# Six raw weight buffers in place of four, four tiles fewer in the common pool, and one addition of a join moved up

## The chip, the cores and the metric

The kernel runs on one core of one Trainium2 chip. The metric is device time in microseconds (us) of one execution, as the median of several runs. TensorE multiplies matrices, VectorE (DVE in the rows) and ScalarE (ACT) work elementwise, GpSimd (POOL) does little here, and SyncE (SP) issues nearly all transfers from the chip's memory.

## The reference

One decoder layer on 256 tokens of width 2048, in float32. Two feed-forward layers of inner width 5632 stand around a mixer (sparse attention and a recurrent branch); this is the part that the change is about:

```python
def swiglu(h, w_in, w_out):
    a, b = jnp.split(h @ w_in, 2, axis=-1)
    return (jax.nn.silu(a) * b) @ w_out

h = layer_norm(DN_ALPHA * h + 0.5 * swiglu(h, ffn1_w_in[l], ffn1_w_out[l]), ln1_g[l], ln1_b[l])
# ... the mixer: q, k, v, indexer, gates, recurrence, three output products ...
h = layer_norm(DN_ALPHA * h + 0.5 * swiglu(h, ffn2_w_in[l], ffn2_w_out[l]), ln3_g[l], ln3_b[l])
```

## The kernel before

**Weights.** Every weight comes in pieces of 128 x 1024 float32 (512 KB). The class `Weights` handles a piece in three steps. `load_to` has SP issue the transfer into a tile named `raw` (`RAW_BUFS` = 4 of them, lines 192 and 206) or, for certain quarters of the feed-forward weights, into tiles named `k` (tags `k0` and `k1`, 4 and 3 of them, line 192). `split_to` turns the piece into a high part `wh` on ACT (line 300) and a low part `wl` = piece minus `wh` on DVE (line 301); there are five tiles of each (`HL_BUFS`). TensorE then takes three products for each operand: `wh` times high, `wl` times high, `wh` times low (lines 734, 735 and 736). A `raw` tile is free for the next transfer when the `wl` of its piece, or the last addition that reads it, has ended.

**Sums of quarters.** For three quarters of a feed-forward block's depth the kernel multiplies by sums of weight quarters instead of the plain quarters. These sums are made in place in the `k` tiles by DVE, `k += k` or `k += raw` (`add`, line 222), and are then split like any other piece. In the rows, `k<-k,raw` is such an addition.

**A feed-forward layer.** `blocksW` runs over 11 blocks of the inner width, in an order written out in `PLAN`: the products of forms P1, P2, Q3 to Q5, P6 and P7 (two groups of three matmuls to a piece), the plain pieces (`c`, twelve matmuls), and fills (`o`, twelve matmuls, line names `ob<-wh,gh`), which multiply the block before by the output weights. At the end of a block, `plain` joins it: two Silu on ACT, two additions `u` and `d` of a product sum in PSUM, two multiplications by the Silu (all lines 819). Just after it the next block's P1 sum is copied, negated, into a new PSUM tile by ACT (`mm<-bp`, line 819), and the form P6 adds to that tile (`mm<-wh,sh`).

**What sets the order.** TensorE, SP and GpSimd run in the order of the code. On DVE and ACT a scheduler sets the order at build time by priority and by its own estimate of when operands are ready; at run time each engine goes through its list in that order and waits where it must. SP too stands still at the first transfer whose tile isn't free, and all that are behind it wait with it.

**The common pool.** Tiles of 128 x 512 float32 that live for a while (activations, `sh`/`sl`, `zs`, `xg`, `vw`, `yr` and others) share one pool of `U_BUFS` = 53.

Of the kernel before, what the change touches and what calls it, by code (L numbers as in the profile page):

```python
# [12 lines left out]
OP = mybir.AluOpType  # L13
# [37 lines left out]

LAG = 2

U_BUFS = 53
T_BUFS = 8
RAW_BUFS = 4
K0_BUFS = 4
K1_BUFS = 3
HL_BUFS = 5
# [85 lines left out]
class Weights:  # L145
# [33 lines left out]
    def load_to(self, i):  # L179
        nc = self.nc  # L180
        while self.loaded <= min(i, len(self.pieces) - 1):
            ap, form = self.pieces[self.loaded]
            k = self.key(self.loaded)
            if isinstance(form, tuple):
                if form[0] in QUARTERS:
# [4 lines left out]
                    else:  # L190
                        t = self.pool.tile([P, PIECE], F32, name=f"raw{self.loaded}", tag="raw", bufs=RAW_BUFS)
                    nc.sync.dma_start(t, ap)
                    self.quarter[form[1], j] = t
            elif k not in self.raw:
# [5 lines left out]
                else:  # L200
                    t = self.pool.tile([P, PIECE], F32, name=f"raw{self.loaded}", tag="raw", bufs=RAW_BUFS)
                if form in QUADS.values():
# [52 lines left out]
    def small(self, name):  # L255
        return self.pool.tile([P, 512], F32, name=name, tag="u", bufs=U_BUFS)

# [119 lines left out]
def tile_layer(ctx, tc, x_fm, x_tm, pos, f1a, f1o, wA, wki, wB, wG, lru, lru_x, wab, wrb, wo, f2a, f2o,  # L377
# [5 lines left out]
    V, A, T, G = nc.vector, nc.scalar, nc.tensor, nc.gpsimd  # L383
    count = [0]

    def name(s):
        count[0] += 1
        return f"{s}{count[0]}"

    def U(s="u", dt=F32):  # L390
        return pool.tile([P, 512], dt, name=name(s), tag="u", bufs=U_BUFS)

# [12 lines left out]
    def CB():  # L405
        return psum.tile([P, 512], F32, name=name("mm"), tag="mm", bufs=2)
# [14 lines left out]
    def BP():  # L421
        return psum.tile([P, 512], F32, name=name("bp"), tag="bp", bufs=4)
# [303 lines left out]
    def blockB(x):  # L726
        ps = MM()
        for k in range(len(x)):
            mmB(ps, x[k], W.unit(P), k == 0, k == len(x) - 1)
        return ps  # L730

    def three(ps, xh, xl, w, start, stop, seeded=False):
        h, l = (v.rearrange("p (a h c) -> p a c h", h=2, c=P) for v in w)
        T.matmul(ps, xh, h, start=start, stop=False, skip_group_check=seeded)  # L734
        T.matmul(ps, xh, l, start=False, stop=False, skip_group_check=seeded)  # L735
        T.matmul(ps, xl, h, start=False, stop=stop, skip_group_check=seeded)  # L736

    def tokens(ps, x, t, w, start, stop, seeded=False):
        h, l = x(t) if callable(x) else (x[:, i, t * P:(t + 1) * P] for i in range(2))
        three(ps, h, l, w, start, stop, seeded)  # L740

    def eager(x, ps):

        ln, x.halves = x.halves, None
        W.step = 512
        base = W.cur + 1
        W.limit = base + AHEAD
        ws = []  # L750
        n = len(ps(0))
        for i in range(8):
            if i == 6:
                ln.half(1)
            ws.append(W.unit(512))
            tokens(ps(0)[i % n], ln.first[i // n], 0, ws[i], i < n, False)
        W.step = PIECE
        for i in range(8):
            tokens(ps(1)[i % n], x[i // n], 1, ws[i], i < n, False)
            if i % 2:  # L760
                W.split_to(base + AHEAD + 1 + i // 2)
        W.limit = None
# [45 lines left out]
    def xop(x, q, i, t):  # L808
        def op(r):
            v = x[4 * q + 2 * r + i]  # L810
            return v[:, 0, t * P:(t + 1) * P], v[:, 1, t * P:(t + 1) * P]
        return op

    def sop(forms, q, i):
        return lambda r: tuple(v[:, i * P:(i + 1) * P] for v in forms[2 * q + r])

    def urgent(f, *args, **kw):
        with tc.high_priority():
            f(*args, **kw)  # L819

    def blocksW(x, forms, fill, done):

        last = {(n, f): i for i, (n, f, k) in enumerate(PLAN)}
        bank = {n: {} for n in range(NBK)}
        z = {n: {} for n in range(NBK)}  # L830
        c = [None, None]

        def banks(t):
            if not c[t]:
                c[t] = [(CB, OB)[t]() for _ in range(2)]
            return c[t]

        def first(k, end):
            ws = [W.unit(512) for _ in range(2)]
            for t in range(2):  # L840
                for j in range(2):
                    tokens(banks(t)[j], x[k], t, ws[j], k == 0, k == NK - 1)
            for t in range(2 if end else 0):
                s = U("z")
                urgent(A.activation, s, c[t][0], AF.Silu)
                urgent(V.tensor_tensor, s, s, c[t][1], op=OP.mult)
                done(0, t, s)

        def plain(n, k, end):
            ws = [W.unit(512) for _ in range(2)]  # L850
            for t, j, b in ((0, 0, "B"), (0, 1, "D"), (1, 1, "A"), (1, 0, "E")):
                tokens(bank[n][b], x[k], t, ws[j], False, end, True)
            if end:
                v, ps = z[n], bank[n]
                s = [U("zs"), U("zs")]
                urgent(A.activation, s[0], ps["B"], AF.Silu)
                urgent(A.activation, s[1], ps["E"], AF.Silu)
                urgent(V.tensor_tensor, v["u"], ps["D"], v["u"], op=OP.add)
                urgent(V.tensor_tensor, v["u"], v["u"], s[0], op=OP.mult)
                done(n, 0, v["u"])  # L860
                urgent(V.tensor_tensor, v["d"], ps["A"], v["d"], op=OP.add)
                urgent(V.tensor_tensor, v["d"], v["d"], s[1], op=OP.mult)
                done(n, 1, v["d"])
                del bank[n], z[n]

        def product(n, form, k, end):
            b, op = {"P1": ("B", xop(x, k, 0, 0)), "P2": ("B", xop(x, k, 1, 0)), "Q3": ("D", sop(forms, k, 3)),
                     "Q4": ("E", xop(x, k, 1, 1)), "Q5": ("D", sop(forms, k, 0)), "P6": ("A", sop(forms, k, 1)),
                     "P7": ("A", sop(forms, k, 2))}[form]
            ps = bank[n]  # L870
            new = b not in ps
            if new:
                ps[b] = BP()
            for r in range(2):
                three(ps[b], *op(r), W.unit(512), new and r == 0, end and r == 1, form not in ("P1", "Q5"))
            if not end:
                return
            if form == "P1":
                ps["A"] = CB()
                urgent(A.activation, ps["A"], ps["B"], AF.Copy, scale=-1.0)  # L880
            elif form == "Q5":
                z[n]["d"] = U("zd")
                urgent(A.activation, z[n]["d"], ps["D"], AF.Copy)
            elif form == "P6":
                z[n]["u"] = U("zu")
                urgent(A.activation, z[n]["u"], ps["A"], AF.Copy)
            elif form == "P7":
                ps["E"] = CB()
                urgent(A.activation, ps["E"], ps["A"], AF.Copy, scale=-1.0)

        skip = 0
        if getattr(x, "halves", None):
            eager(x, banks)
            skip = 4
        for i, (n, form, k) in enumerate(PLAN):
            end = i == last[n, form]
            if i < skip:
                continue
            if form == "o":
                fill()  # L900
            elif n == 0:
                first(k, end)
            elif form == "c":
                plain(n, k, end)
            else:
                product(n, form, k, end)
# [18 lines left out]
    def column_block(x, forms, plan):  # L925


        if plan:
            return blockM(x, forms, plan)
        return [[p] for p in blockA(x)]  # L930
# [360 lines left out]
    qT, kT, v, qiT = [None] * 8, [None] * 2, [None] * 2, [None] * 4  # L1291
# [182 lines left out]
    for b in a_order:  # L1474
# [9 lines left out]
        ps = blockA(hs)  # L1484
# [16 lines left out]
    for nb in range(4):  # L1501
        if WGA and nb == WGA[0]:
            forms = make_forms(hs, QG)
        ps = column_block(hs, forms, MIXED["wG"].get(nb))
# [6 lines left out]
    for nb in range(4):  # L1511
        ps = column_block(ya, forms, MIXED["wab"].get(nb))
# [91 lines left out]
    for j in range(NR + LAG):  # L1604
# [5 lines left out]
        if j < NR:  # L1610
            ps = blockB(hs)
# [15 lines left out]
            ps = blockB(hs)  # L1627
# [3 lines left out]
        if j >= LAG:  # L1631
# [7 lines left out]
            if c == TPG - 1:  # L1639
                ps = BP()  # L1640
# [31 lines left out]
    for nb in range(4):  # L1672
        if WO and nb == 3:
            mforms = make_forms(mg, U)
        ps = column_block(yr, forms, MIXED["wrb"].get(nb))
        for t in range(2):
            d = gr[nb][t]
# [115 lines left out]
```

## Time and profile before

| | |
|---|---|
| runs | 2251.0, 2253.88, 2257.98 us (median 2253.88) |
| the profiled execution | 2250.04 us, of which its span is 2248.2 us |
| TensorE busy | 2219.8 us (99%) |
| DVE, ACT busy | 1958.7 us (87%), 1559.6 us (69%) |
| DMA | 459.33 MB, mean 204 GB/s |
| feed-forward layers | about 0 to 680 us and 1570 to 2240 us of the span |

A timeline row reads: start and duration in us, engine, line, operation, output <- inputs, shapes, count; in brackets the idle time of the engine just before it and what ended that. A row of waits reads: who waited, at which line, for whom: us in total, times, longest. Matmuls overlap: each lasts 0.38 us in the rows, but in an undisturbed stretch they start 0.216 us apart (0.21 and 0.22 in the rows), so TensorE's pace is read from the starts.

### The profile page before, as it was taken

What the parts mean: (1) busy time and instruction counts of PE and PEld (TensorE: products, weight loads), DVE (VectorE), ACT (ScalarE), POOL (GpSimd) and SP (SyncE); (2) the same over time, 40 slices, a digit from 0 to 9 for tenths busy, and PEclk for the clock granted to TensorE, in tenths of its full rate; (3) what the DMA queues carried; (4) which work ended last, traced back from release to release, by engine and by line L of the source; (5) the groups of instructions that cost most, each with busy time, mean ns of one, the idle gap of its engine ahead of it and who ended that gap; (6) DMA issues with size and microseconds to landing.
All of it is one profiled execution on the core that took longest, in us unless ns stands there. A gap on an engine that the chain in (4) does not pass through costs nothing.

```text
span 2248.2 us, 30930 instructions
## 1 busy us (share of the span) xinstructions
PE 2219.8 (99%) x11164; PEld 1939.3 (86%) x11164; DVE 1958.7 (87%) x2617; ACT 1559.6 (69%) x2222; POOL 22.4 (1%) x58
## 2 busy tenths in 40 slices
PE   9999999999999999999999999999999999999999
PEld 8888888888888888889999888898888888888887
DVE  7899999999988887678788886898999999999997
ACT  6777777777766556555688885555777777777774
POOL 0000000000001000000000000000000000000000
PEclk9999999999999999999999999999999999999999
DMA  8666655566666555566655566556666656665664
GB/s 302 215 225 218 205 192 203 197 204 215 211 206 219 175 182 164 161 214 199 209 177 188 184 203 235 194 194 195 215 220 210 219 199 223 220 209 193 206 213 157
DMA packets 133498, 459.33 MB, mean 204 GB/s; under 512 B 15040, under 2 KB 17856, under 8 KB 133344
## 3 DMA queue, kind: packets, MB, share of 16 engines
q1 hardware_dynamic: 130608, 449.37, 59.9%
q0 software_dynamic: 2160, 6.94, 1.0%
q8 instruction: 87, 1.43, 0.3%
q10 hardware_dynamic: 576, 1.05, 0.1%
q14 instruction: 67, 0.55, 0.1%
HBM read 455.20 MB, written 2.10 MB: 203 GB/s over the span
## 4 chain that ended last, share of the span: by engine, by line
PE 62%; DVE 17%; DMA 8%; issue 7%; ACT 5%; POOL 0%; ACTq 0%; SPq 0%; DVEq 0%; POOLq 0%
DVE wl L301 11%; PE ob L735 8%; PE ob L736 7%; PE ob L734 7%; PE mm L734 7%; PE mm L735 7%; PE mm L736 7%; DVE k L222 4%; DMA raw<-f2a 4%; DMA raw<-f1a 4%; PE bp L736 3%; PE bp L734 3%; PE bp L735 3%; ACT wh L300 3%; PE ob L723 2%
## 5 line engine op out<-in xcount | busy, mean ns | idle before, releaser
L301 DVE TENSOR_TENSOR wl<-raw,wh 128x1024 fp32r<-128x1024 f32 (+2 forms) x734 | 858.2, 1184 | 137.6 <-ACT wh L300 132.6
L300 ACT ACTIVATE wh<-raw 128x1024 fp32r<-128x1024 f32 (+2 forms) x734 | 741.4, 1025 | 320.0 <-PE mm L736 127.1
L301 DVE TENSOR_TENSOR wl<-k,wh 128x1024 fp32r<-128x1024 f32 x290 | 349.3, 1220 | 37.3 <-ACT wh L300 35.3
L300 ACT ACTIVATE wh<-k 128x1024 fp32r<-128x1024 f32 x290 | 302.7, 1056 | 112.4 <-DVE k L222 55.0
L735 PE MATMUL ob<-wl,gh 128*128 128x512 f32 x640 | 244.4, 382 | 9.8 <-DVE wl L301 9.8
L734 PE MATMUL ob<-wh,gh 128*128 128x512 f32 x640 | 244.6, 382 | 1.4 <-ACT ob L1226 1.4
L736 PE MATMUL ob<-wh,gl 128*128 128x512 f32 x640 | 242.7, 379 | 0.0
L222 DVE TENSOR_TENSOR k<-k,raw 128x1024 f32<-128x1024 f32 x174 | 211.6, 1219 | 32.0 <-DMA raw<-f1a 16.5
L734 PE MATMUL mm<-wh,hs 128*128 128x512 f32 x418 | 161.6, 387 | 0.0
L736 PE MATMUL mm<-wh,hs 128*128 128x512 f32 x418 | 158.5, 379 | 0.4 <-DVE hs L1054 0.4
L735 PE MATMUL mm<-wl,hs 128*128 128x512 f32 x418 | 158.5, 379 | 0.2 <-DVE wl L301 0.2
L735 PEld LDWEIGHTS ob<-wl,gh 128*128 128x128 f32 x640 | 121.0, 189 | 33.0 <-DVE wl L301 17.0
L734 PEld LDWEIGHTS ob<-wh,gh 128*128 128x128 f32 x640 | 121.0, 189 | 19.2 <-ACT ob L1226 2.8
L736 PEld LDWEIGHTS ob<-wh,gl 128*128 128x128 f32 x640 | 121.0, 189 | 17.1 <-DVE gl L819 0.5
L1238 ACT ACTIVATE y<-ob 128x512 f32<-128x512 f32 x152 | 89.5, 590 | 65.8 <-PE ob L736 65.7
L734 PE MATMUL ob<-wh,hs 128*128 128x512 f32 x304 | 118.4, 390 | 1.0 <-ACT hs L1053 1.0
L736 PE MATMUL ob<-wh,hs 128*128 128x512 f32 x304 | 115.5, 380 | 0.6 <-DVE hs L1054 0.6
L735 PE MATMUL ob<-wl,hs 128*128 128x512 f32 x304 | 115.2, 379 | 0.0
L723 PE MATMUL ob<-hs,wh 128*128 128x512 f32 x336 | 111.2, 382 | 0.0
L734 PE MATMUL bp<-wh,sh 128*128 128x512 f32 (+1 forms) x298 | 107.8, 362 | 1.3 <-ACT zd L819 1.3
L723 PE MATMUL mm<-hs,wh 128*128 128x512 f32 x320 | 106.7, 384 | 0.0
L735 PE MATMUL bp<-wl,sh 128*128 128x512 f32 (+1 forms) x298 | 106.1, 356 | 0.0
(404 smaller groups left out, 4828.2 us busy)
## 6 DMA issues: line engine op xcount, KB each, us to landing
raw<-f2a SPq DMA_DIRECT2D x118, 512.0 KB, 4.3
raw<-f1a SPq DMA_DIRECT2D x116, 512.0 KB, 4.5
raw<-f1o SPq DMA_DIRECT2D x88, 512.0 KB, 4.2
raw<-f2o SPq DMA_DIRECT2D x88, 512.0 KB, 3.7
raw<-wB SPq DMA_DIRECT2D x80, 512.0 KB, 4.5
raw<-wA SPq DMA_DIRECT2D x64, 512.0 KB, 3.5
raw<-wG SPq DMA_DIRECT2D x64, 512.0 KB, 3.6
k<-f1a SPq DMA_DIRECT2D x58, 512.0 KB, 6.9
```

Of the source, the lines that this page charges most:

```text
L222: self.nc.vector.tensor_tensor(v, v, self.quarter[q, j], op=OP.add)
L300: nc.scalar.activation(hp, src, AF.Copy)
L301: self.last = nc.vector.tensor_tensor(lp, src, hp, op=OP.subtract)
L723: T.matmul(ps, w[0], turns(x.rearrange("p a t -> p (a t)")), start=first, stop=False)
L734: T.matmul(ps, xh, h, start=start, stop=False, skip_group_check=seeded)
L735: T.matmul(ps, xh, l, start=False, stop=False, skip_group_check=seeded)
L736: T.matmul(ps, xl, h, start=False, stop=stop, skip_group_check=seeded)
L1238: A.activation(Y[t][nb], open_ps[t], AF.Copy, scale=0.5)
```

## The change

`RAW_BUFS` goes from 4 to 6, `U_BUFS` from 53 to 49 (a `raw` tile is twice as large as one of the pool, so the memory stays the same), and in the join the addition of `d` is written ahead of the addition of `u`.

```diff
-U_BUFS = 53
+U_BUFS = 49
 T_BUFS = 8
-RAW_BUFS = 4
+RAW_BUFS = 6
...
                 urgent(A.activation, s[1], ps["E"], AF.Silu)
+                urgent(V.tensor_tensor, v["d"], ps["A"], v["d"], op=OP.add)
                 urgent(V.tensor_tensor, v["u"], ps["D"], v["u"], op=OP.add)
                 urgent(V.tensor_tensor, v["u"], v["u"], s[0], op=OP.mult)
                 done(n, 0, v["u"])
-                urgent(V.tensor_tensor, v["d"], ps["A"], v["d"], op=OP.add)
                 urgent(V.tensor_tensor, v["d"], v["d"], s[1], op=OP.mult)
```

The order of TensorE, SP and GpSimd stays row for row. That of DVE and ACT is set by the scheduler. Three places of one block of the first feed-forward layer stand here (in the other blocks it is the same pattern); the numbers in the names tell tiles apart.

DVE, some pieces ahead of a join (`k_110`, `k_112`, `k_113` hold quarters, `raw_2120` is the quarter that two of them take up):

```order
 L301 TENSOR_TENSOR wl_2057<-k_110_1966,wh_2056 128x1024
 L301 TENSOR_TENSOR wl_2069<-k_113_2010,wh_2068 128x1024
+L222 TENSOR_TENSOR k_110_1966<-k_110_1966,raw_2120 128x1024
+L222 TENSOR_TENSOR k_113_2010<-k_113_2010,k_114_2022 128x1024
 L222 TENSOR_TENSOR k_108_1935<-k_108_1935,raw_2066 128x1024
-L222 TENSOR_TENSOR k_113_2010<-k_113_2010,k_114_2022 128x1024
+L222 TENSOR_TENSOR k_112_1997<-k_112_1997,raw_2120 128x1024
 L301 TENSOR_TENSOR wl_2094<-k_113_2010,wh_2093 128x1024
 L301 TENSOR_TENSOR wl_2104<-raw_2041,wh_2103 128x1024
```

Two additions more now stand ahead of `wl_2094`: four in a row in place of two.

DVE at the join itself, a few rows on:

```order
 L301 TENSOR_TENSOR wl_2133<-k_105_1898,wh_2132 128x1024
 L301 TENSOR_TENSOR wl_2147<-raw_2091,wh_2146 128x1024
-L222 TENSOR_TENSOR k_110_1966<-k_110_1966,raw_2120 128x1024
 L819 TENSOR_TENSOR zu_1797<-bp_1531,zu_1797 128x512
 L819 TENSOR_TENSOR zd_1635<-mm_1620,zd_1635 128x512
```

The addition of `raw_2120` is gone from ahead of the join. The join's additions stand as before, `u` first: the scheduler keeps that order in all 20 joins, so the line that the diff moves moves no instruction.

ACT at the same place, with what each row waits for (this order is the same before and after):

```order
L819 ACTIVATE zs_2179<-mm_1923 128x512 [waits PE_49]
L300 ACTIVATE wh_2188<-k_110_1966 128x1024 [waits DVE_49,Activation_49]
L819 ACTIVATE mm_2142<-bp_2009 128x512 [waits Activation_49]
L300 ACTIVATE wh_2204<-raw_2120 128x1024 [waits DMAHW2_49,PE_49]
L300 ACTIVATE wh_2218<-raw_2144 128x1024 [waits DMAHW3_49,PE_49]
```

Nothing moved here. The copy `mm_2142<-bp_2009` waits for ACT's own earlier rows alone, the last of which is the split of `k_110`, and that one waits for DVE's addition.

DVE ahead of the piece of a fill, some 20 us after the join:

```order
 L301 TENSOR_TENSOR wl_2310<-raw_2249,wh_2309 128x1024
-L222 TENSOR_TENSOR k_105_1898<-k_105_1898,raw_2216 128x1024
+L222 TENSOR_TENSOR k_110_1966<-k_110_1966,raw_2321 128x1024
 L301 TENSOR_TENSOR wl_2324<-k_108_1935,wh_2323 128x1024
-L222 TENSOR_TENSOR k_110_1966<-k_110_1966,raw_2321 128x1024
 L222 TENSOR_TENSOR k_113_2010<-k_113_2010,raw_2345 128x1024
 L301 TENSOR_TENSOR wl_2348<-raw_2280,wh_2347 128x1024
```

One addition has gone from here to an earlier row; the addition of `raw_2345` still stands right ahead of the fill's `wl_2348`.

## The prediction

> **What bounds the kernel now.** I read the busy times first, then who waited for whom on TensorE, then the timelines of DVE, ACT and SP around those waits, and last the DMA rates.
>
> ```profile
> PE 2219.8 (99%) x11164; PEld 1939.3 (86%) x11164; DVE 1958.7 (87%) x2617; ACT 1559.6 (69%) x2222; POOL 22.4 (1%) x58
> PE ob L735 <- DVE wl L301: 9.8, 16, 1.1
> PE mm L734 <- ACT mm L819: 5.5, 9, 1.2
> PEld mm L734 <- ACT mm L819: 11.6, 15, 1.6
> ```
>
> TensorE is the bound, and nearly all of its idle time behind an engine is in two kinds of wait: a fill waits for the low part of its weights (first row of waits), and P6 waits for ACT's copy into its PSUM tile (the other two). A change to buffers can win these waits and no more. How much are they in the steady blocks? The same view for 100 to 600 us gives the first two rows, for 1680 to 2150 us the last two:
>
> ```profile
> PE ob L735 <- DVE wl L301: 4.0, 6, 0.9
> PE mm L734 <- ACT mm L819: 2.7, 5, 0.7
> ```
>
> ```profile
> PE ob L735 <- DVE wl L301: 4.2, 7, 0.9
> PE mm L734 <- ACT mm L819: 2.8, 4, 1.2
> ```
>
> Idle time understates the loss, since a matmul lasts 0.38 us in the rows but the next may start after 0.216. One wait of each kind, from TensorE's timeline:
>
> ```profile
> 261.30 0.38 PE L734 MATMUL ob<-wh,gh 128*128 128x512 f32 x1
> 262.59 0.48 PE L735 MATMUL ob<-wl,gh 128*128 128x512 f32 x1 [0.92 <-DVE wl L301]
> 262.91 0.38 PE L736 MATMUL ob<-wh,gl 128*128 128x512 f32 x1
> ```
>
> ```profile
> 238.54 0.38 PE L736 MATMUL ob<-wh,gl 128*128 128x512 f32 x1
> 239.59 0.48 PE L734 MATMUL mm<-wh,sh 128*128 128x512 f32 x1 [0.67 <-ACT mm L819]
> 239.91 0.38 PE L735 MATMUL mm<-wl,sh 128*128 128x512 f32 x1
> ```
>
> From 261.30 to 262.91 two steps took 1.61 us instead of 0.43: 1.18 lost for 0.92 of idle. From 238.54 to 239.91 it is 1.37 - 0.43 = 0.94 for 0.67. So each wait costs its idle time and 0.26 more. Fills: 4.0 + 4.2 + 13 x 0.26 = 11.6 us. P6: 2.7 + 2.8 + 9 x 0.26 = 7.8 us, and the six waits that only the weight load shows (15 against 9) at an estimated 0.3 each, 1.8: together 9.6 us. Both: 21.2 us.
>
> **Where these waits come from.** DVE and ACT around the first of them, the block of the order rows above:
>
> ```profile
> 224.11 1.23 DVE L222 TENSOR_TENSOR k<-k,raw 128x1024 f32<-128x1024 f32 x1 [0.96 <-DMA raw<-f1a]
> ...
> 231.00 1.22 DVE L301 TENSOR_TENSOR wl<-k,wh 128x1024 fp32r<-128x1024 f32 x1 [1.12 <-ACT wh L300]
> ...
> 236.68 1.22 DVE L222 TENSOR_TENSOR k<-k,raw 128x1024 f32<-128x1024 f32 x1
> ...
> 257.31 1.22 DVE L222 TENSOR_TENSOR k<-k,raw 128x1024 f32<-128x1024 f32 x1
> 260.18 1.23 DVE L222 TENSOR_TENSOR k<-k,raw 128x1024 f32<-128x1024 f32 x1 [1.65 <-DMA raw<-f1a]
> 261.32 1.22 DVE L301 TENSOR_TENSOR wl<-raw,wh 128x1024 fp32r<-128x1024 f32 x1
> ```
>
> ```profile
> 236.58 0.58 ACT L819 ACTIVATE zs<-mm 128x512 f32<-128x512 f32 x1
> 237.99 1.06 ACT L300 ACTIVATE wh<-k 128x1024 fp32r<-128x1024 f32 x1 [0.83 <-DVE k L222]
> 238.96 0.58 ACT L819 ACTIVATE mm<-bp 128x512 f32<-128x512 f32 x1
> ```
>
> The issues of the quarters added at 236.68 and 260.18, on SP, and the totals of who waited for what:
>
> ```profile
> 233.39 0.33 SPq L192 DMA_DIRECT2D raw<-f1a  x1
> ```
>
> ```profile
> 255.15 0.33 SPq L192 DMA_DIRECT2D raw<-f1a  x1
> ```
>
> ```profile
> SPq L206 <- DVE wl L301: 1091.2, 414, 9.9
> ```
>
> ```profile
> DVE k L222 <- DMA raw<-f1a: 16.5, 19, 2.0
> DVE k L222 <- DMA raw<-f2a: 14.3, 18, 1.7
> ```
>
> The fill's wait is a late transfer: DVE stood 1.65 us for a quarter (at 260.18), then added, then made the fill's `wl` (261.32 to 262.54), and TensorE went on at 262.59. P6's wait is the same at one remove: ACT stood 0.83 us until DVE had added `raw_2120` into `k_110` (236.68), and the copy for P6 stood behind that in ACT's order. The transfers are late because SP waits for a free `raw` tile: the quarter added at 236.68 went out at 233.39, that of 260.18 at 255.15. The totals of SP's stands behind `wl` (1091.2 us) and of DVE's behind quarters (16.5 and 14.3 us in 37 cases) say that this is the rule.
>
> **The change part by part.**
>
> *Six raw buffers.* A transfer waits for the release of the sixth tile back instead of the fourth. The built program names the slots: `raw_2120` follows the piece whose `wl` is the first row below, `raw_2345` that of the second.
>
> ```profile
> 218.08 1.23 DVE L301 TENSOR_TENSOR wl<-raw,wh 128x1024 fp32r<-128x1024 f32 x1
> ```
>
> ```profile
> 250.50 1.22 DVE L301 TENSOR_TENSOR wl<-raw,wh 128x1024 fp32r<-128x1024 f32 x1
> ```
>
> So `raw_2120` can go out at 219.3 instead of 233.4, and `raw_2345` at 251.7 instead of 255.15, a row sooner still if DVE is ahead. SP's issue costs 0.33 us a transfer and hides in its stands; there is no transfer more than before.
>
> *The moved additions.* DVE makes 1.135 us a row in this stretch (231.00 to 236.68 is five rows). Before: from the addition at 224.11, five rows, then the 1.12 us for ACT, then `wl_2094` at 231.00. After: seven rows, no stand. If the quarter of 224.11 comes in time, that addition starts at 223.1 (the 0.96 and the 0.08 by which rows overlap), and `wl_2094` at 223.1 + 7 x 1.135 = 231.0: the same. What TensorE has to spare there is small (below). With `raw_2120` added by 227.7 instead of 237.9, ACT splits `k_110` right behind the Silu of 236.58, at 237.1, and copies at 238.0 instead of 238.96: P6, which came 0.63 us behind the copy, could start at 238.7, and TensorE wants it at 238.54 + 0.216 = 238.76. The 0.94 us are gone, with 0.1 to spare. What is late next: nothing in ACT's order there but the copy itself.
>
> *The fill.* The join begins one row sooner, at 236.8 instead of 237.8, and one addition more (`k_112`) has left the rows behind it, so DVE reaches the addition of `raw_2345` at 258.5 - 1.0 - 1.1 = 256.3 (258.5 is the end of the row at 257.31). The transfer, issued at 250 to 252, took 5.0 us from issue to addition before (255.15 to 260.18) and lands at 255 to 257. `wl_2348` then starts at 257.5 to 258.2 instead of 261.32, 3 us sooner for a wait of 1.18: gone as well. Total so far -21.2 us.
>
> *The join's line.* Nothing: its rows stand as before, and P6's copy does not wait for them, as its list of waits showed.
>
> *Four pool tiles fewer.* The trace has no row for a tile that isn't there, so I bound it. Laid over this trace's times, the new slots leave every tile's first write behind the end of the slot's last user, but for eight in the recurrent branch with under 1.5 us between them, of this sort:
>
> ```profile
> 1285.91 0.66 DVE L994 TENSOR_TENSOR yr<-xg,yr 128x256 fp32r<-128x256 f32 x1
> ```
>
> ```profile
> 1286.66 0.47 ACT L1589 ACTIVATE vw<-bp,hba 128x256 f32<-128x256 f32 x1
> ```
>
> The `vw` of 1286.66 takes the slot that the row above it reads to 1286.57. Lower end 0; upper end one DVE row of 1.2 us in each of eight, 9.8 us, if all reached TensorE. I take 0.5 us, near the lower end, since all eight times are positive.
>
> *The sum.* 2250.0 - 21.2 + 0.5 is 2229.3 for the profiled execution's own time, and I add 1 us for waits of a tenth or two that appear in 18 blocks with so little to spare. That is 20 us off; on the median of 2253.9, 3.8 us above this execution, 2234.
>
> **What speaks against it: the burst of transfers.** The loads of the next quarters go out together, and now two more `raw` ones follow them at once.
>
> ```profile
> 268.00:284.00 16.00, 16.00 (x76) 14.01 (x75) 14.50 (x13) 11.06 (x12) 0.00 (x0) 1.00 0.94 346
> ```
>
> ```profile
> 285.24 1.23 DVE L222 TENSOR_TENSOR k<-k,raw 128x1024 f32<-128x1024 f32 x1 [0.82 <-DMA raw<-f1a]
> ```
>
> The DMA engines were 94% busy from 268 to 284 us, at 346 GB/s. In this stretch the `k` loads of a block go out as the block before gives their tiles free; with six buffers the quarter that was late at 285.24 becomes the eighth load of a burst that I reckon from 270.1, the first of these releases. At 346 GB/s eight times 524 KB take 12.1 us, to 282.2; a lone load of at most 3.3 us (233.39 to 236.68), less 1.5 for its bytes, leaves 1.8 for the rest of its way, so it lands at about 284.0 (270.1 + 12.1 + 1.8). DVE wants it at 285.24 - 0.82 - 0.08 = 284.3. It fits, barely. The Trainium skill, "DMA: Bandwidth & Descriptors", section "Queues, rings and completion order", says that each engine takes descriptors in ring order, so a load issued earlier isn't served ahead of the burst; the trace agrees, with 94% busy in that stretch. By that page's fit (section on the anatomy of one DMA), 2.0 us plus the bytes at 436 GB/s, the eighth would land after an estimated 11.6 us, at 281.7, which leaves 2.6 us and the same sum.
>
> **The rivals.**
>
> *Slower: four additions in a row ahead of `wl_2094`.* That row ended at 232.22, and TensorE took it at 232.50:
>
> ```profile
> 232.50 0.38 PE L735 MATMUL bp<-wl,sh 128*128 128x512 f32 x1
> ```
>
> The fill's wait above shows 0.05 us as the least between the two, so 0.23 us is to spare. If the quarter ahead of them lands x later than in this trace, `wl_2094` is x + 1.07 us late (two rows more, 2.27, less the 1.20 of ACT's stand and its overlap), and TensorE loses x + 0.84 in each of 18 blocks. At x = -1.04, my forecast, nothing; at x = -0.34, one microsecond later than I reckon, 9 us, a sum of 2243; at x = 0, 15 us, 2249; from x = 0.33 on the gain is eaten, and at 0.8 it is 2262.
>
> *Half:* only the fill's or only P6's wait goes, because the other is bound by something that this trace hides (ACT's copy has 0.1 us to spare): 10 to 12 us off, 2242 to 2244.
>
> *No change:* the transfers are earlier but TensorE's time is the sum of its matmuls and of small stands that form anew, 2250 to 2257, the range of the runs. For it: TensorE is at 99%. Against it: the 21 us above are gaps between starts, each with its own cause.
>
> *Slower by the pool:* 9.8 us at its upper end; alone it can't outweigh the gain.
>
> **How the numbers follow.** My forecast 0.62, 2226 to 2240 (a gain of 14 to 25 and some 3 us of scatter in the runs). The two kinds of half gain (x near -0.34, or one wait left) 0.18, 2241 to 2247. No change, with x between 0 and 0.5, 0.12. The slower rival 0.08. A measurement of this kernel can tell about 0.3%, 6.8 us: faster is below 2247.1, slower above 2260.6. So faster 0.62 + 0.18 = 0.80, same 0.12, slower 0.08. The range 2226 to 2247 leaves out the last two cases.
>
> **What would show it.** Right: DVE's stands at line 222 for `raw` fall from 31 us to a few; the two rows of TensorE's waits almost vanish from the steady blocks; the blocks repeat 21.2 / 18 = 1.2 us sooner. DVE's 87% rises a little, since its work is the same in less time. Wrong: TensorE's wait moves to `bp` at line 735 behind `wl` ahead of the join (the burst), or rows of L1589, L993 and the matmuls at 1270 to 1340 us show new stands (the pool). My argument fails most easily at the landing time of the eighth load, which is known to no better than 1 us.

## The result, and the profile after

The changed kernel takes 2226.35 us (median of four runs, 2225.74 to 2226.66), the kernel before 2253.23 us on the same count of runs (2251.0 to 2257.98): a ratio of 0.9878, with a 95% interval of 0.986 to 0.9895. That is 27 us off where 20 were forecast. The profiled execution takes 2225.74 us, its span is 2223.9, so 24.3 us less than the one before. The page's first part after the change:

```profile
PE 2211.6 (99%) x11164; PEld 1942.6 (87%) x11164; DVE 1953.6 (88%) x2617; ACT 1559.2 (70%) x2222; POOL 22.4 (1%) x58
```

TensorE's busy share reads 99% as before, and says nothing of the 24 us. The Trainium skill, "Perfetto Trace Analysis", section "Identifying the Most-Contended Engine", warns that the matmul's busy share is no measure of the room left, and points to the weight loads' share; the trace agrees: that one went from 86 to 87%. Who waited for whom tells more. First DVE, at line 222, over the whole span:

```profile
DVE k L222 <- DMA raw<-f1a: 1.5, 1, 1.5
DVE k L222 <- DMA raw<-f2a: 1.2, 1, 1.2
```

37 stands of 30.8 us have become two of 2.7 us. TensorE's longest waits, over the whole span:

```profile
PE ob L734 <- ACT ob L1226: 1.4, 2, 0.7
PE ob L735 <- DVE wl L301: 1.1, 1, 1.1
PE ob L734 <- ACT hs L1053: 1.0, 3, 0.5
PE bp L515 <- POOL tri L492: 1.0, 1, 1.0
```

The one fill that still waits for `wl` is at 1610 us, at the start of the second feed-forward layer; from 100 to 600 and from 1680 to 2150 us no wait of TensorE for another engine is left. P6's wait for ACT's copy is gone from the list.

The block of the prediction again. It now runs 3.7 us earlier at the join and 4.4 earlier at the fill. DVE and ACT up to the join:

```profile
223.02 1.22 DVE L222 TENSOR_TENSOR k<-k,raw 128x1024 f32<-128x1024 f32 x1
224.16 1.22 DVE L222 TENSOR_TENSOR k<-k,k 128x1024 f32<-128x1024 f32 x1
225.29 2.35 DVE L222 TENSOR_TENSOR k<-k,raw 128x1024 f32<-128x1024 f32 x2
227.57 1.22 DVE L301 TENSOR_TENSOR wl<-k,wh 128x1024 fp32r<-128x1024 f32 x1
...
233.24 0.68 DVE L819 TENSOR_TENSOR zu<-bp,zu 128x512 f32<-128x512 f32 x1
```

```profile
232.92 0.60 ACT L819 ACTIVATE zs<-mm 128x512 f32<-128x512 f32 x1 [0.56 <-PE mm L736]
233.42 1.05 ACT L300 ACTIVATE wh<-k 128x1024 fp32r<-128x1024 f32 x1
234.36 0.59 ACT L819 ACTIVATE mm<-bp 128x512 f32<-128x512 f32 x1
```

The four additions stand in a row and none waits; ACT splits the `k` tile right behind the second Silu and copies. P6 and the fill on TensorE, and DVE ahead of the fill:

```profile
235.10 0.38 PE L736 MATMUL ob<-wh,gl 128*128 128x512 f32 x1
235.31 0.38 PE L734 MATMUL mm<-wh,sh 128*128 128x512 f32 x1
...
256.91 0.38 PE L734 MATMUL ob<-wh,gh 128*128 128x512 f32 x1
257.13 0.38 PE L735 MATMUL ob<-wl,gh 128*128 128x512 f32 x1
```

```profile
252.74 1.22 DVE L222 TENSOR_TENSOR k<-k,raw 128x1024 f32<-128x1024 f32 x1
253.87 1.22 DVE L301 TENSOR_TENSOR wl<-raw,wh 128x1024 fp32r<-128x1024 f32 x1
```

Both places keep TensorE's step of 0.21 to 0.22 us. Before it was 1.05 us at P6 and 1.29 at the fill. The transfers behind it, on SP: `raw_2120`, then `raw_2345` with its time to landing (the last column), then the quarter at the end of the burst that the slower rival spoke of, with its time to landing and its addition:

```profile
215.89 0.33 SPq L192 DMA_DIRECT2D raw<-f1a  x1
```

```profile
247.17 0.33 SPq L192 DMA_DIRECT2D raw<-f1a  x1
...
raw<-f1a SPq DMA_DIRECT2D x1, 512.0 KB, 3.3
```

```profile
269.08 0.48 SPq L192 DMA_DIRECT2D raw<-f1a  x1
```

```profile
raw<-f1a SPq DMA_DIRECT2D x1, 512.0 KB, 9.4
```

```profile
278.77 1.22 DVE L222 TENSOR_TENSOR k<-k,raw 128x1024 f32<-128x1024 f32 x1
```

Over all 116 quarters that go into `raw` tiles, the median time from the issue on SP to the addition on DVE has risen from 4.7 to 9.0 us. The last of the burst landed at 269.08 + 9.4 = 278.5, and its addition began at 278.77 without a stand.

### The profile page after: what moved, and what is told of

It reads as the page before. It is cut to its first block, busy times and chain, and to the rows that moved or that the text cites. A ratio compares the mean times of both kernels' runs of the same rounds, so it can differ in the third digit from the quotient of the medians.

```text
span 2223.9 us, 30910 instructions
## 1 busy us (share of the span) xinstructions
PE 2211.6 (99%) x11164; PEld 1942.6 (87%) x11164; DVE 1953.6 (88%) x2617; ACT 1559.2 (70%) x2222; POOL 22.4 (1%) x58
## 3 DMA queue, kind: packets, MB, share of 16 engines
q10 hardware_dynamic: 576, 1.05, 0.1%
## 4 chain that ended last, share of the span: by engine, by line
PE 91%; DVE 3%; ACT 3%; issue 2%; DMA 1%; POOL 0%; ACTq 0%; SPq 0%; DVEq 0%; POOLq 0%
PE ob L734 11%; PE ob L735 11%; PE ob L736 11%; PE mm L734 10%; PE mm L735 10%; PE mm L736 10%; PE bp L735 6%; PE bp L734 6%; PE bp L736 6%; PE ob L723 2%; PE mm L723 2%; DVE wl L301 1%; PE ob L724 1%; PE mm L724 1%; ACT wh L300 1%
```

## The experiments

Two theories stood at first. *Transfers*: the gain comes from quarters that have landed when their addition is due. *Order*: it comes from the place of the additions in DVE's list, above all from the one that left its place ahead of the join.

**1. The join's line undone.** Six buffers, 49 pool tiles, the join as before.

```diff
-U_BUFS = 53
+U_BUFS = 49
-RAW_BUFS = 4
+RAW_BUFS = 6
```

> Six raw buffers and 49 pool tiles, the join written as before (u first). The built order of every engine is row for row that of the changed kernel. If the join's line is inert, 2226 us, within 1 us of the changed kernel, and the runs lie within 2 us of each other. If the line mattered in some way that the order of rows doesn't show, more than 2 us off.

Measured: 2225.27 us (2225.09 to 2225.69), ratio 0.9879 (0.9864 to 0.9894). The line is inert, and the two numbers of buffers alone make the whole difference. Since every engine runs the rows of the changed kernel, the 1.1 us between the two medians is what two sets of runs of one order can differ by.

**2. Six buffers with the old order.** Each addition at line 222 is given a dependency without a semaphore on the `wl` behind which it stood before. In the steady feed-forward blocks DVE then has the rows of the kernel before. The code is shortened.

```diff
-U_BUFS = 53
+U_BUFS = 49
-RAW_BUFS = 4
+RAW_BUFS = 6
...
-        self.nc.vector.tensor_tensor(v, v, self.quarter[q, j], op=OP.add)
+        a = self.nc.vector.tensor_tensor(v, v, self.quarter[q, j], op=OP.add)
+        self.tc.add_manual_dep(a, self.wls[-1 - BEHIND[self.adds]], NoSync)
```

> Six raw buffers and 49 pool tiles, but each of VectorE's additions into a k tile is held behind the same wl as in the kernel before, so that VectorE's order in the feed-forward blocks is the old one; only the transfers are earlier. Theory 'transfers' (the gain comes from quarters that land in time; the moved additions are only the scheduler's answer to them): with no stand for the quarter of 224.11 everything behind it on VectorE is 0.96 us earlier, the addition ahead of the join ends at 236.9 instead of 237.9, which is just enough for P6, and the fill has 2 us to spare: 2226 to 2230 us, the two waits of TensorE nearly gone. Theory 'order' (P6's wait goes because the addition left its place ahead of the join): P6's copies stay late, about 8 to 10 us of 27 are not won: 2234 to 2238 us, with the rows of mm behind ACT still in the waits. If order were everything: 2250.

Measured: 2225.03 us (2224.34 to 2225.91), ratio 0.9878 (0.9864 to 0.9891). DVE's stands at line 222 over the whole span, its rows ahead of the join, and ACT's:

```profile
DVE k L222 <- DMA raw<-f2a: 0.7, 1, 0.7
```

```profile
232.17 1.22 DVE L222 TENSOR_TENSOR k<-k,raw 128x1024 f32<-128x1024 f32 x1
233.31 0.69 DVE L819 TENSOR_TENSOR zu<-bp,zu 128x512 f32<-128x512 f32 x1
```

```profile
233.48 1.07 ACT L300 ACTIVATE wh<-k 128x1024 fp32r<-128x1024 f32 x1
234.45 0.59 ACT L819 ACTIVATE mm<-bp 128x512 f32<-128x512 f32 x1
```

The addition stands ahead of the join as it used to, ends at 233.39, and ACT goes on 0.09 us later, 0.06 us behind the changed kernel. TensorE starts this P6 at 235.30 without a stand; in the whole kernel one P6 still waits for ACT's copy, 0.4 us. The theory 'order' has fallen. The gain is that of the transfers, and the moved additions are neither needed for it nor do they harm it.

**3. Five buffers, 51 pool tiles.**

> Five raw buffers, 51 pool tiles: half of the dose. VectorE's order in the blocks is nearly that of the changed kernel (four additions in a row ahead of wl_2094). The fifth buffer lets raw_2120 go out near 222 instead of 233.4 (the sixth: 219.3), and raw_2345 one row or two ahead of 255.15. Theory 'transfers', with the time set by whether a quarter is there when its addition comes up: 2228 to 2236 us, VectorE's stands for raw at 2 to 10 us instead of 31 (before) and 3 (after). If the two tiles counted alike: about 2240. If five with the longer row of additions ahead of wl_2094 is the bad mixture that the slower rival spoke of: 2245 to 2255, with a new wait of bp at line 735.

Measured: 2226.32 us (2225.51 to 2226.74), ratio 0.9883 (0.9869 to 0.9896). The first added buffer brings all of it; I had expected 2 to 10 us less. DVE's stands at line 222 show that five are only just enough:

```profile
DVE k L222 <- DMA raw<-f2a: 6.0, 11, 1.5
DVE k L222 <- DMA raw<-f1a: 3.1, 10, 0.7
```

Of these 9.1 us little reaches TensorE: its starts of `bp` at line 735, behind `wl`, come 1.2 us later in sum than with six buffers. That is the place of the slower rival.

**4. The smaller pool alone.** Four `raw` buffers, 49 pool tiles.

> Four raw buffers as before, 49 pool tiles: the price of the pool alone. Forecast 0.5 us (upper end 9.8): 2251 to 2255 us, and no new wait at the rows of the recurrent branch. On the spread of the runs: if it comes from the late transfers, these runs spread over 4 us or more, as the four of the kernel before did (2251.0 to 2258.0), while the kernels with six buffers stay within 2 us; if it comes from the chip, all kernels of this call spread alike.

Measured: 2254.97 us (2252.5 to 2260.36, eleven runs), ratio 1.0012 (1.0003 to 1.0021): about 2.7 us, where 0.5 was forecast. The extra does not stand in the recurrent branch: from the last fill of the first layer to the first fill of the second TensorE takes 954.7 us with either pool. TensorE's two waits for late quarters are there as before:

```profile
PE ob L735 <- DVE wl L301: 9.0, 12, 2.0
PE mm L734 <- ACT mm L819: 7.7, 11, 1.9
```

**5. How much there is to spare.** In experiments 5 to 7 useless transfers, whose data nobody reads, go out ahead of each quarter that is loaded into a `raw` tile, to push the end of the burst. The first two hold each addition between the two `wl` between which it stands in the changed kernel, the third between those of the kernel before. The rest of the order is the scheduler's, and it isn't quite the old one: in experiments 5 and 6 the four additions ahead of `wl_2094` have another order among themselves, and in experiment 6 some rows at the join have moved. The code is shortened.

```diff
+                        for j in range(1):    # experiment 5; 2 in experiments 6 and 7
+                            nc.sync.dma_start(self.small("dm"), ap[:, j * 512:(j + 1) * 512])
                     nc.sync.dma_start(t, ap)
```

> The changed kernel with one useless transfer of 256 KB put ahead of each of the 116 quarters that go into raw tiles (into a pool tile that nobody reads), VectorE's order in the blocks held to that of the changed kernel. 256 KB are 0.75 us at 346 GB/s, and SP's issue adds 0.33. Theory 'margin' (quarters are issued a median of 9 us ahead of their addition, a lone one needs 3.3, so a microsecond is to spare): 2226 to 2229 us. Theory 'brink' (the prediction's slower rival, with four additions ahead of wl_2094 and only 0.3 us of the burst to spare): x rises by about 1, TensorE loses up to 0.8 us in each of 18 blocks, 2236 to 2242 us, as waits of bp at line 735.

Measured: 2229.64 us (2228.94 to 2231.12), ratio 0.989 (0.9874 to 0.9906). 3.3 us are lost, nearly all of it in a wait that stands in the list of neither kernel:

```profile
PE bp L735 <- DVE wl L301: 2.7, 6, 0.9
```

**6. Twice the load.**

> The same with two useless transfers of 256 KB ahead of each quarter: 1.5 us of bytes and 0.66 us of issues, about twice that where two quarters go out in one burst. Theory 'margin': the quarters of the burst were issued 9.4 to 9.7 us ahead of their addition and now need about 9; those issued 5.6 us ahead are late by 1 to 2 us, but the fill behind them has 2 to 3 us to spare: 2226 to 2236 us, likeliest 2229. Theory 'brink': x = +1, that is 18 times 1.8: 2258 us or more.

Measured: 2238.04 us (2237.6 to 2238.92), ratio 0.9927 (0.9912 to 0.9943). The same wait, the block of the prediction (the quarter's issue with its time to landing, DVE, TensorE):

```profile
PE bp L735 <- DVE wl L301: 10.0, 12, 1.5
```

```profile
210.88 0.44 SPq L192 DMA_DIRECT2D raw<-f1a  x1
```

```profile
raw<-f1a SPq DMA_DIRECT2D x1, 512.0 KB, 9.8
```

```profile
220.66 1.23 DVE L222 TENSOR_TENSOR k<-k,raw 128x1024 f32<-128x1024 f32 x1 [1.38 <-DMA raw<-f1a]
...
228.62 1.21 DVE L301 TENSOR_TENSOR wl<-k,wh 128x1024 fp32r<-128x1024 f32 x1
```

```profile
228.42 0.38 PE L734 MATMUL bp<-wh,sh 128*128 128x512 f32 x1
229.89 0.48 PE L735 MATMUL bp<-wl,sh 128*128 128x512 f32 x1 [1.09 <-DVE wl L301]
```

This is the slower rival, step by step: a late quarter (1.38 us), the additions in a row, a late `wl`, 1.25 us lost on TensorE. Its price was right: a stand of 1.38 is x = 1.38 - 1.04 = 0.34, for which the prediction gives 0.34 + 0.84 = 1.18 us. Neither forecast had the size of the whole, 11.7 us: 'brink' expected 32 us of loss, 'margin' 3. The step of 'brink' that failed is the delay: with x = 1 in every block DVE would have stood 2 us for a quarter, but it stood 16.0 us in 17 places, so 0.9 us each.

**7. The same load, the old order of the additions.**

> The same two useless transfers, but VectorE's additions held to the order of the kernel before (two of them ahead of wl_2094, that of raw_2120 right ahead of the join). Theory 'margin': within 3 us of the run with the new order. Theory 'brink': since fewer additions stand ahead of wl_2094, it loses less there: at least 10 us faster than the run with the new order.

Measured: 2234.27 us (2233.5 to 2235.89), ratio 0.9909 (0.989 to 0.9928). The wait of `bp` is nearly gone (0.5 us, against 10.0 in experiment 6), and one of the fills has come in its place:

```profile
PE ob L735 <- DVE wl L301: 7.0, 10, 1.1
```

This is 3.8 us better than experiment 6, between what the two theories said. It isn't the price of the additions' order alone, though. The additions stand between the same `wl` as in the kernel before, but that of `raw_2120` is behind the join and not ahead of it, and ACT now copies for P6 ahead of the split that waits for this addition:

```profile
235.08 0.58 ACT L819 ACTIVATE mm<-bp 128x512 f32<-128x512 f32 x1
238.23 1.06 ACT L300 ACTIVATE wh<-k 128x1024 fp32r<-128x1024 f32 x1 [2.57 <-DVE k L222]
```

What the two runs show is that, where quarters are late, the number of additions ahead of a `wl` decides which `wl` pays for them. How much of the 3.8 us that is worth, and how much ACT's moved copy, they don't separate.

**8. Five buffers with the old order**, held as in experiment 2.

> Five raw buffers, 51 pool tiles, VectorE's additions held to the order of the kernel before. With five buffers and the scheduler's own order the waits of bp behind wl at line 735 took 1.2 us more than with six. If those come from the four additions in a row (the slower rival in small), they go here: 1.9 us of lost starts there instead of 3.2, and 2224 to 2226 us. If they come from late transfers alone, they stay, or the waits of P6 and of the fills come back by a few us: 2226 to 2232 us.

Measured: 2225.51 us (2225.17 to 2226.14), ratio 0.9872 (0.9856 to 0.9887). DVE's stands at line 222 are down from 9.1 to 1.4 us, and the 1.2 us that five buffers had cost at `bp`, line 735, are gone. As times, 2225.5 and 2226.3 can't be told apart; the traces say that the additions moved to the front ask for their quarters sooner than five buffers can bring them, and that the old order does not.

**9. Five buffers, 49 pool tiles**, to see whether experiment 4's loss is the pool's own.

> Five raw buffers, 49 pool tiles: against the run with five and 51, two pool tiles fewer and nothing else (the orders differ only in some 40 rows of the recurrent branch). With four raw buffers the smaller pool measured 0.1% slower, but its extra waits stood in the feed-forward blocks, at late quarters. If the pool itself costs 2 to 3 us, this kernel takes 2228 to 2229 us. If that cost was one of late transfers alone, which are gone here: 2225 to 2227 us, and the excess at 1250 to 1350 us unchanged.

Measured: 2225.32 us (2224.8 to 2227.7), ratio 0.9886 (0.9869 to 0.9902). With quarters nearly in time (DVE stands 6.8 us for them) the pool costs nothing that can be measured. Why four buffers with the small pool are a little slower than with the large one is not settled.

None of these kernels is more than 1.3 us faster than the changed one, and the one with the same order of every engine, experiment 1, is 1.1 us faster. Four buffers with the order of the changed kernel were not run, and by the rows they can't be had: before, `raw_2120` went out at 233.39, when the `wl_2104` of 232.14 had ended, and in the new order its addition stands ahead of that `wl`.

## Why the prediction was right in kind and short in size

**What held.** The two waits that it named were the gain, and went for the reason given. `raw_2120` was to go out at 219.3 in the old trace's time: 215.89 + 3.66 (the Silu at 236.58 before, at 232.92 after) is 219.55. `raw_2345` was to go out at 251.7: 247.17 + 4.39 (the fill's first row at 261.30 before, 256.91 after) is 251.56. The `wl` of the fill was to start at 257.5 to 258.2: 253.87 + 4.39 is 258.26. Four additions in a row were to leave 0.2 us at `wl_2094`: it ended at 228.79, and TensorE took it at 229.05:

```profile
229.05 0.38 PE L735 MATMUL bp<-wl,sh 128*128 128x512 f32 x1
```

**The burst.** The eighth load was to land 0.3 us ahead of its addition, and it did: 278.5 against 278.77. The time from the first issue of the burst, 264.50, to this landing is 14.0 us, and the prediction's own rows gave 12.1 + 1.8 = 13.9. That they agree so well is partly luck: the last five of the eight landed 1.27 to 1.29 us apart, which is 410 GB/s and not 346, and the third landed 2.9 us behind the second. The fit of the Trainium skill, "DMA: Bandwidth & Descriptors", section on the anatomy of one DMA, gave an estimated 11.6. The page states that fit for a single transfer issued by GpSimd; for the last of eight issued by SP the measurement decides against it. The first load of the burst, a `k`, did nearly as the fit says, 3.4 us against 2.0 + 1.2 = 3.2:

```profile
264.50 0.33 SPq L192 DMA_DIRECT2D k<-f1a  x1
```

```profile
k<-f1a SPq DMA_DIRECT2D x1, 512.0 KB, 3.4
```

The prediction took DMA engines that are 94% busy as a sign that loads are served in the order of their issue. A busy share can't show an order, but the landings do: in both traces the 907 transfers of SP landed in the order in which they were issued.

**The rivals.** The slower one is real but did not set in; experiments 5 and 6 reached it with a little added traffic. *Half* and *no change* fell with the waits. The pool as a loss of its own fell with experiment 9 and with the mixer's time below. *Order*, which the prediction had taken as part of the mechanism (P6 "gone" because the addition left the join), was not needed: in experiment 2 the addition stands ahead of the join, and P6 is in time.

**Which step failed.** The mechanism held, and the sum was too small: 20 us on the median, where 27 were measured. Two steps of it failed: the count of the waits, and the 3.8 us of scatter put on top of them. Both kernels run the same 11164 matmuls in the same order, so each step from one start to the next can be set against the same step before. Together the steps are 24.29 us shorter, which is the difference of the spans. By terms:

| term | forecast, us | measured, us |
|---|---|---|
| fills (`ob` at lines 735 and 736) | -11.6 | -13.20 |
| P6 (`mm` at 734 to 736) | -9.6 | -10.33 |
| first block's join wait (`bp` at 734, 58 us) | 0 | -1.34 |
| the mixer (forecast as the pool's) | +0.5 | 0.00 |
| new small waits, and the rest | +1.0 | +0.58 |
| sum for the profiled execution | -19.7 | -24.29 |

The mixer, from the last fill of the first layer to the first fill of the second, takes TensorE 954.74 us in both kernels and 954.6 to 954.9 us in all experiments, with 53, 51 and 49 pool tiles.

The price of a wait, its idle time and 0.26, was right. What was short is the count: I took the waits from 100 to 600 and from 1680 to 2150 us and left out the ends of both layers, and a wait for which the profile shows no idle time can still delay a start. In the row of the fills' `wl`, 16 starts lost 0.15 us or more before that lose none after, where I had counted 13. "Nearly all of its idle time" was too much said as well: the list over the whole span has 23.0 us, and the two kinds of wait make 15.3. Of the rest I put everything at nothing, and one wait went too, the first block's. It stood in the profile before, and I did not ask what it came from:

```profile
PE bp L734 <- ACT zd L819: 1.3, 1, 1.3
```

ACT's copy stood there behind a split that had waited 1.18 us for an addition on DVE, much as at P6.

Of the nearly 8 us between the 2234 forecast and the 2226.35 measured, the terms of the table make 4.6. Another 3.2 are the step from the execution to the median. I added 3.8 us, since the median stood so far above the profiled execution before, as if that were scatter that any version has. The changed kernel's median is 0.6 us above its profiled execution. The kernel before ran from 2248.8 to 2259.8 us over 33 runs; the five kernels with five or six buffers and no useless load, 20 runs in all besides the changed kernel's own four, stayed between 2224.3 and 2227.7. The wide spread belongs to the kernels with four buffers (experiment 4 has it too, 2252.5 to 2260.4). It isn't late quarters as such: experiment 6 has many, and its four runs spread over 1.3 us. Nor does the granted clock account for it: the runs before whose clock reads 1.0 lie between 2248.8 and 2256.4. What makes it is open; a loop in which a late addition frees its tile late and so delays the next quarter would do it, but no run here shows that. With the waits undercounted and this scatter added, the median came to lie at the low end of the forecast, 2226 to 2240, and not in its middle.

## What to carry to other kernels

Read the lead of a transfer, from its issue to its first use, against its time to landing: with a median lead of 4.7 us late quarters cost 24 us, with 9.0 next to nothing, and the 6.7 that one buffer more gives were enough. Price the waits from the starts of all matmuls and not from the list of idle times, and don't take the scatter of a kernel that waits for transfers over into the forecast for one that doesn't. Before crediting a scheduler's new order, hold the old one under the new buffers: here the new order was worth nothing that could be measured.

## What the hardware showed that was not expected

The same 512 KB took 3.3 us as a lone load and 9.4 us as the eighth of a burst, both counted from its own issue. A useless 256 KB ahead of each quarter cost only 3.3 us in 2226, with 7% more bytes moved (116 times 262 KB, 30 of 459 MB), and twice as much cost 11.7: with a quarter's lead at 9 us, the first 7% of added traffic cost 3.3 us and the next 7% 8.4.
